# Releasing the second block's attention of a pair after the first part of that block's value projection

## The chip, the cores and the metric

The kernel runs on one core of a Trainium2 chip. Its time is the device time in microseconds (us) of one execution; the figure for a kernel is the median of its runs. The core has five engines that run their own instruction queues in order and wait for one another by semaphores: TensorE (PE in the profile, with PEld for its weight loads), VectorE (DVE), ScalarE (ACT), GpSimd (POOL) and SyncE (SP), which here issues the DMA transfers.

## The reference

One decoder block on 2048 tokens with 1024 features. Sliding-window attention and an mLSTM branch run side by side on one combined projection, then comes a SwiGLU feed-forward part. Cut to what matters here:

```python
h = modulate(rms_norm(x, g_pre_mix[l]), shift_m, scale_m)
proj = h @ w_in[l]
q_a, k_a, v_a, q_m, k_m, v_m, o_m, i_m, f_m, g_a, g_m = jnp.split(proj, split_points, axis=-1)
q_a = rope(q_a.reshape(B, S, N_Q_HEADS, HEAD_DIM), positions)      # 8 heads of 64
k_a = rope(k_a.reshape(B, S, N_KV_HEADS, HEAD_DIM), positions)     # 2 heads
y_a = sliding_window_attention(q_a, k_a, v_a, attn_sinks[l])       # window 128, blocks of 128
...
h_m = mlstm_chunkwise(q_m, k_m, v_m, i_pre, f_pre)
...
merged = sigmoid(g_a) * (y_a @ w_branch_attn[l]) + sigmoid(g_m) * (y_m @ w_branch_mlstm[l])
x = x + gate_m[:, None, :] * rms_norm(merged @ w_out[l], g_post_mix[l])
... # feed-forward part
```

In one attention block 128 queries meet the 128 keys of their own block and the 128 before:

```python
s = jnp.einsum('bnqhgd,bnkhd->bnhgqk', qb, kb)
m = jnp.maximum(jnp.max(s, axis=-1, keepdims=True), sink)
p = jnp.exp(s - m)
p = p / (jnp.sum(p, axis=-1, keepdims=True) + jnp.exp(sink - m))
o = jnp.einsum('bnhgqk,bnkhd->bnqhgd', p, vb)
```

## The kernel before

The tokens are cut into four blocks of 512, and these into two pairs. `superblock(sb)` writes the mixer part of one pair, with blocks b0 and b1; the feed-forward part follows after both pairs. Each operand of a large product is held as two terms, a rounded value and the rest, so that one product is three matmuls.

For each block three projections are made by `token_group`: q, kv (keys, values and gate inputs) and vm (the value rows of the mLSTM, function `vm`). A group yields four parts for vm; a part is 24 matmuls with 512 columns (128x512 in the profile, tile acc), and each of the four PSUM banks of the pool acc is evacuated when its 128 tokens are done (L819 for vm, L773 for q, L798 for kv), into tiles of the pool tx (nine buffers). Of the first pair's first block some steps are written in another function. After the projections of both blocks come the pair's other projections, `om`, `qk`, `ga`, `gm`, in a form with seven products for eight (tiles acc<-big,hl, with casts at L1588 on ACT and subtractions at L1589 on DVE), and then the outputs of b0 and of b1. The sums that this form needs of the hidden rows are made by `hsums` (casts L535 on ACT), of which one pair of sums is spawned before the projections of b1 and one behind them, by `start_f`.

Everything else is side work, written as generators ("streams") that yield how long they want to be left alone: `q_stream` and `k_stream` (transposes after the rotation, results stored to at_d in HBM), `gates(b)`, two attention streams, the convolution and the mLSTM chunks. While `run2` writes the matmuls of the parts, each advances an estimated clock `now[0]`, and `tick` lets each stream that is due write its next step:

```python
for _ in it.mms(made.pop(done)):
    if it.weave:
        tick()
```

A function among the items (`yield lambda: attend(b1)`) is called when `run2` comes to it. A scheduler then sets the final order of each engine's queue from this program, so the order on each engine is not simply the order of writing.

Attention of 128 tokens (`attention(n)`, n from 0 to 15, four to each block of 512) is: load the operands (L900, SP, at<-at_d; two buffers at), two groups of twelve score matmuls (L211, mix<-at, 64x256; two head groups on the two halves of PE's rows), copies to tm (L923, L925), exponentials on ACT (L938), a multiplication on POOL (L942), eight transposes (L216, mix<-ident,tm), four products with the values (L211, mix<-tm,at) and the store of the result. A bank of the pool mix (four) holds each of these results in PSUM. Two streams take the even and the odd attention blocks in turn; both may go on as far as `ready[0]` says:

```python
def attention_stream(u):
    for i in range(u, 2 * NT, 2):
        while i >= ready[0]:
            yield 1000.0
        yield from attention(b0 * NT + i)
...
def attend(b):
    finish(R["qk"])
    ready[0] = (b - b0 + 1) * NT
    if b == b0:
        R["att"] = [spawn(attention_stream(0), L_QK), spawn(attention_stream(1), L_QK + L_ATT2)]
    R["gs", b] = [spawn(gates(b), L_QK)]
```

So `attend(b1)` first has all steps written that the rotated q and k of b1 still owe, then lets the streams go on to the last four attention blocks of the pair (4 to 7, or 12 to 15), and spawns the gates of b1. The attention results of b1 are read after `end_attention(2 * NT)`, ahead of b0's output projection; the gates after the projection `qk` 3.

Of the kernel before, what the change touches and what calls it, by code (L numbers as in the profile page):

```python
# [72 lines left out]
def decoder_block(ctx: ExitStack, tc: tile.TileContext, a: dict, out: bass.AP, dbg=None):  # L73
# [49 lines left out]
    def tx(shape, dtype=F32):  # L123
        return tpool.tile(shape, dtype, tag="tx", name=nm("tx"), bufs=9)
# [93 lines left out]
    def spawn(gen, delay=0.0):  # L218
        st = [now[0] + delay, gen, False]
        streams.append(st)  # L220
        return st
# [15 lines left out]
    def finish(sts):  # L237
        for st in sts:
            while not st[2]:
                now[0] = max(now[0], min(q[0] for q in streams))  # L240
                tick()
# [75 lines left out]
    def token_group(srcs, nk, n, lhs, evac, pair_heads=False, stagger=1):  # L317

        acc = []
        srcs = list(srcs)  # L320
        held = []

        def make(si, k0, kc):
            def mms(wt):
                if not acc:
                    acc.extend(acc_tile() for _ in range(NT))
                held.append((wt, k0, kc))
                if len(srcs) - stagger <= si < len(srcs) - 1:
                    return
                for t in range(NT):  # L330
                    for w_, k0_, kc_ in held:
                        for j in range(kc_):
                            kk = k0_ + j
                            mm3(acc[t][:, :n], lhs(kk, t), (w_[0][:, j, :], w_[1][:, j, :]), kk == 0, kk == nk - 1)
                            yield
                    if si == len(srcs) - 1:
                        evac(t, acc[t])
                held.clear()
            return mms

        for si, (raw, view, k0, kc) in enumerate(srcs):
            yield piece(raw, view, [kc, n], make(si, k0, kc), pair_heads)

    def srcs_rows(w, nk, c0):
        for k0 in range(0, nk, 4):
            kn = min(4, nk - k0)
            raw = raw_rows(w, k0, kn, c0)
            for j in range(0, kn, 2):
                yield raw, (lambda t, j=j: t[:, j:j + 2, :]), k0 + j, 2
# [48 lines left out]
    b1 = const.tile([P, 48], F32, name="b1")  # L398
# [125 lines left out]
    def hsums(names):  # L524

        for name in names:
            raw = HR.pop(name)
            lo = hc_part(name, 1)
            nc.sync.dma_start(lo.bitcast(F32), raw)
        yield L_HD  # L530
        for name in names:
            hi, lo = (hc_part(name, i) for i in range(2))
            for k in range(4):
                v = lo[:, k, :].bitcast(F32)
                A.copy(hi[:, k, :], v)  # L535
                V.tensor_tensor(lo[:, k, :], v, hi[:, k, :].bitcast(F32), op=ALU.subtract)
                yield L_HS
# [190 lines left out]
    def superblock(sb):  # L728
        b0, b1 = 2 * sb, 2 * sb + 1
        R = {}  # L730

        def lhs_h(b):
            def lhs(kk, t):
                return tuple(p_[:, kk % 4, t * P:(t + 1) * P] for p_ in HC[f"{kk // 4 + 1}{b % 2 + 1}"])
            return lhs
# [80 lines left out]
        def vm(b):  # L816
            def evac(t, ps):
                v = tx([P, 512])
                A.copy(v, ps)  # L819
                nc.sync.dma_start(vm_d[b][:, t, :], v)  # L820
            yield from token_group(srcs_rows(w_in, KD, C_VM), KD, 512, lhs_h(b), evac)
# [149 lines left out]
# [5 lines that stand above are left out]
                done_att[0] += 1  # L976
                yield 500.0
# [3 lines left out]
# [6 lines that stand above are left out]
# [305 lines left out]
        q1, kv1 = (list(z) for z in q_kv(b1))  # L1292
        yield from kv1
        yield from q1
        yield from vm(b1)

        def start_f():
            finish([hps["t"]])
            HC.pop("12")
            hps["t"] = spawn(hsums(("T1", "T3")))  # L1300
            attend(b1)

        yield start_f
        pairs = [("om", 0), ("qk", 0), ("om", 1), ("qk", 1), ("ga", 0), ("qk", 2), ("ga", 1), ("qk", 3),
# [740 lines left out]
    def program():  # L2045
        items = [it for sb in range(NSB) for it in superblock(sb)]
        last = max(i for i, it in enumerate(items) if isinstance(it, Part))
        first_block()
        yield from items[:last]
        yield lambda: next(phase2)  # L2050
        yield from items[last:]
# [47 lines left out]
```

## Time and profile before

| | |
|---|---|
| median of 3 runs | 2695.2 us (2694.12 to 2695.24) |
| profiled execution | 2696.74 us, span 2695.0 us |
| mean granted clock of TensorE | 0.992 |
| busy: PE, DVE, ACT, POOL | 98%, 74%, 48%, 5% of the span |
| first pair, 190 to 560 us | PE busy throughout |
| second pair, 740 to 880 us | PE busy 126.94 of 140 us |

Rows of the timeline give the start and the time from the first start to the last end of a run of like instructions (us), engine, line, operation, output<-input, shapes and count; in brackets the idle time of the engine ahead of it and what ended it. Since matmuls overlap, a run's cost is the distance to the next start. Windows give busy times of each engine between two times, the granted clock (1.00 is full) and the share of time in which the 16 DMA engines were busy. Line numbers are those of the kernel before; behind line 1300 the changed kernel's are higher by 2.

### The profile page before, as it was taken

To read this page: it belongs to the slowest core of one execution; us is meant where nothing else is said; L and a number is where in the kernel's file an instruction comes from. 1 tells how busy PE (TensorE), PEld (TensorE's weight loads), DVE (VectorE), ACT (ScalarE), POOL (GpSimd) and SP (SyncE) were. 2 spreads that over 40 slices of the span, in tenths; PEclk is the share of its full clock that TensorE was granted. 3 is DMA by queue.
4 is the path that set the end of the run, shared out by engine and by line. 5 is a ranking of instruction groups with operands and counts; after the bars stand their busy time and mean duration, and the time that the engine had idled before them with its cause. 6 is when DMAs were issued, how large, how long until landed. Compare 5 with 4: busy or idle time off the path is not lost.

```text
span 2695.0 us, 35854 instructions
## 1 busy us (share of the span) xinstructions
PE 2635.9 (98%) x12382; PEld 2149.4 (80%) x12382; DVE 1986.3 (74%) x3882; ACT 1297.2 (48%) x2525; POOL 136.8 (5%) x181
## 2 busy tenths in 40 slices
PE   7899999999998999999999999999999999999998
PEld 6777788888885778888887888887877888888886
DVE  7888887768686888876687777776677676766466
ACT  4657544545754554444563443334554333333444
POOL 0100001100101000110000000000000000000000
PEclk9999999999998999999999999999999999999999
DMA  7574456897574644677775564436675232324566
GB/s 251 172 236 138 147 176 185 267 341 243 188 246 145 204 139 139 204 250 284 243 233 192 178 201 160 153 118 215 213 272 187 98 118 88 111 98 145 191 207 219
DMA packets 353637, 511.89 MB, mean 190 GB/s; under 512 B 25120, under 2 KB 213660, under 8 KB 348208
## 3 DMA queue, kind: packets, MB, share of 16 engines
q1 hardware_dynamic: 353288, 509.55, 57.2%
q8 instruction: 97, 1.59, 0.2%
q14 instruction: 84, 0.69, 0.1%
q10 hardware_dynamic: 168, 0.06, 0.0%
HBM read 357.12 MB, written 144.02 MB: 186 GB/s over the span
## 4 chain that ended last, share of the span: by engine, by line
PE 84%; DVE 6%; DMA 4%; ACT 2%; issue 1%; POOL 0%; SPq 0%; DVEq 0%; POOLq 0%; ACTq 0%
PE acc L211 59%; PE mix L211 22%; PE mix L216 2%; DVE hl L1589 1%; DMA at_d<-tx 1%; DMA raw<-as_d 1%; DMA tx<-in_w_ada_dram 1%; ACT hl L1588 1%; DMA at<-at_d 1%; DMA raw<-in_w_ffn_down_dram 1%; DVE wlo L267 0%; DMA raw<-ws_d 0%; DMA big<-big 0%; DVE tm L925 0%; DVE big L1589 0%
## 5 line engine op out<-in xcount | busy, mean ns | idle before, releaser
L211 PE MATMUL acc<-big,hl 128*128 128x512 f32 x3936 | 939.5, 393 | 2.3 <-ACT hl L1588 0.9
L211 PEld LDWEIGHTS acc<-big,hl 128*128 128x128 f32 x3936 | 732.8, 188 | 168.5 <-issue 9.0
L1588 ACT CAST hl<-raw 128x512 fp32r<-128x512 f32 x732 | 440.2, 621 | 494.9 <-PE acc L211 227.9
L1589 DVE TENSOR_TENSOR hl<-raw,hl 128x512 fp32r<-128x512 f32 x732 | 497.9, 696 | 196.5 <-ACT hl L1588 194.1
L211 PE MATMUL acc<-whi,big 128*128 128x512 f32 (+1 forms) x1216 | 356.2, 374 | 7.7 <-ACT tx L89 3.8
L211 PE MATMUL mix<-big,hl 128*128 128x512 f32 x1056 | 262.9, 390 | 1.7 <-ACT hl L1588 1.0
L211 PEld LDWEIGHTS acc<-whi,big 128*128 128x128 f32 x1216 | 222.0, 190 | 49.7 <-ACT tx L89 4.3
L211 PE MATMUL acc<-hl,hl 128*128 128x512 f32 x1008 | 237.3, 393 | 5.9 <-DVE hl L1589 3.3
L211 PEld LDWEIGHTS mix<-big,hl 128*128 128x128 f32 x1056 | 197.8, 188 | 44.4 <-ACT hl L1588 1.9
L211 PE MATMUL acc<-wlo,big 128*128 128x512 f32 (+1 forms) x608 | 225.9, 374 | 3.5 <-DVE wlo L267 3.5
L211 PEld LDWEIGHTS acc<-hl,hl 128*128 128x128 f32 x1008 | 187.0, 188 | 51.6 <-DVE hl L1589 8.7
L211 PE MATMUL mix<-hl,hl 128*128 128x512 f32 x792 | 182.3, 390 | 1.2 <-DVE ms L455 0.5
L211 PEld LDWEIGHTS mix<-hl,hl 128*128 128x128 f32 x792 | 148.0, 188 | 34.5 <-DVE hl L1589 2.9
L211 PE MATMUL acc<-big,whi 128*128 128x512 f32 x512 | 157.3, 393 | 0.0
L267 DVE TENSOR_TENSOR wlo<-raw,whi 128x1024 fp32r<-128x1024 f32 (+1 forms) x95 | 108.8, 1146 | 60.4 <-ACT whi L266 54.7
L266 ACT CAST whi<-raw 128x1024 fp32r<-128x1024 f32 (+1 forms) x95 | 93.7, 987 | 116.0 <-PE acc L211 104.7
L211 PEld LDWEIGHTS acc<-wlo,big 128*128 128x128 f32 x608 | 115.6, 190 | 24.1 <-DVE wlo L267 5.0
L457 POOL TENSOR_TENSOR rs<-ms,halves 128x1 f32<-128x1 f32 (+1 forms) x56 | 42.9, 779 | 1657.0 <-DVE ms L455 1647.2
L211 PE MATMUL mix<-hcT4h,hl 128*128 128x512 f32 x352 | 115.6, 389 | 0.7 <-ACT hl L1588 0.7
L211 PE MATMUL acc<-hcT2h,hl 128*128 128x512 f32 x352 | 115.5, 389 | 0.0
L211 PEld LDWEIGHTS acc<-big,whi 128*128 128x128 f32 x512 | 95.3, 188 | 19.2
L211 PE MATMUL acc<-big,wlo 128*128 128x512 f32 x256 | 97.5, 392 | 0.0
(350 smaller groups left out, 3544.2 us busy)
## 6 DMA issues: line engine op xcount, KB each, us to landing
raw<-in_w_in_dram SPq DMA_DIRECT2D x48, 1024.0 KB, 5.6
as_d<-w SPq DMA_DIRECT2D x154, 256.0 KB, 2.0
raw<-as_d SPq DMA_DIRECT2D x70, 512.0 KB, 3.9
raw<-in_w_ffn_gate_dram SPq DMA_DIRECT2D x22, 1024.0 KB, 5.7
raw<-in_w_ffn_up_dram SPq DMA_DIRECT2D x22, 1024.0 KB, 5.5
raw<-ws_d SPq DMA_DIRECT2D x40, 512.0 KB, 4.6
y_d<-tm SPq DMA_DIRECT2D x64, 256.0 KB, 3.7
tx<-in_w_ada_dram SPq DMA_DIRECT2D x64, 256.0 KB, 4.2
```

Of the source, the lines that this page charges most:

```text
L211: T.matmul(o, lhsT=lhsT, rhs=rhs, start=start, stop=stop, skip_group_check=resumed)
L216: T.transpose(o, i, ident[:k, :k])
L266: A.copy(hv, src)
L267: V.tensor_tensor(lv, src, hv.bitcast(F32), op=ALU.subtract)
L457: G.tensor_tensor(r[:, :n], ms[:, :n], nhalf[:, :n], op=ALU.pow)
L1588: A.copy(v(hi), src)
L1589: V.tensor_tensor(v(lo), src, v(hi).bitcast(F32), op=ALU.subtract)
```

## The change

`attend(b1)` is called after the first of the four parts of b1's vm, and no longer in `start_f`, which follows the fourth.

```diff
         yield from kv1
         yield from q1
-        yield from vm(b1)
+        vm1 = list(vm(b1))
+        yield from vm1[:len(vm1) // 4]
+        yield lambda: attend(b1)
+        yield from vm1[len(vm1) // 4:]
 
         def start_f():
             finish([hps["t"]])
             HC.pop("12")
             hps["t"] = spawn(hsums(("T1", "T3")))
-            attend(b1)
 
         yield start_f
```

The number of instructions on each engine stays; their order changes within both pairs, not in the feed-forward part. Three places follow, of before first and then of the changed kernel.

On PE in the first pair, at the first scores of attention block 4 (mix<-at). acc<-whi,big and acc<-wlo,big are matmuls of vm, acc<-big,hl those of the projections behind it:

```order
L211 MATMUL acc_1974<-whi_2063,big_993 128x512
L211 MATMUL mix_2253<-at_2156 128x256
L211 MATMUL mix_2254<-at_2156 128x256
...
L211 MATMUL mix_2253<-at_2156 128x256
L211 MATMUL acc_2145<-big_365,hl_2069 128x512
L211 MATMUL acc_2145<-big_378,hl_2069 128x512
L211 MATMUL mix_2254<-at_2156 128x256
L211 MATMUL acc_2145<-big_365,hl_2069 128x512 x2
```

```order
L211 MATMUL acc_1974<-whi_2035,big_993 128x512
L211 MATMUL acc_1971<-whi_2114,big_992 128x512
L211 MATMUL mix_2142<-at_2045 128x256 x4
L211 MATMUL mix_2143<-at_2045 128x256 x4
L211 MATMUL mix_2142<-at_2045 128x256
L211 MATMUL mix_2143<-at_2045 128x256
L211 MATMUL mix_2142<-at_2045 128x256
L211 MATMUL mix_2143<-at_2045 128x256
L211 MATMUL acc_1971<-wlo_2115,big_992 128x512
```

The twelve scores stood behind vm's last matmul, as eleven and one; they now stand together, 23 of vm's matmuls earlier.

On PE in the second pair, at the value products of attention block 8 (mix<-tm,at) and the transposes of block 9 (mix<-ident,tm):

```order
L211 MATMUL acc_8268<-whi_8356,big_7135 128x512
L211 MATMUL mix_7777<-tm_7755,at_7501 64x512
L216 MATMUL mix_7788<-ident,tm_7665 128x128
L211 MATMUL mix_7777<-tm_7770,at_7501 64x512
L216 MATMUL mix_7788<-ident,tm_7665 128x128 x2
L211 MATMUL mix_7777<-tm_7757,at_7501 64x512
L216 MATMUL mix_7788<-ident,tm_7665 128x128
L211 MATMUL mix_7777<-tm_7772,at_7501 64x512
L216 MATMUL mix_7805<-ident,tm_7666 128x128 x4
L211 MATMUL acc_8268<-wlo_8357,big_7135 128x512
```

```order
L211 MATMUL acc_8266<-wlo_8357,big_7135 128x512
L211 MATMUL mix_7777<-tm_7755,at_7501 64x512
L216 MATMUL mix_7788<-ident,tm_7665 128x128 x4
L216 MATMUL mix_7805<-ident,tm_7666 128x128 x2
L211 MATMUL mix_7777<-tm_7770,at_7501 64x512
L211 MATMUL mix_7777<-tm_7757,at_7501 64x512
L216 MATMUL mix_7805<-ident,tm_7666 128x128
L211 MATMUL mix_7777<-tm_7772,at_7501 64x512
L216 MATMUL mix_7805<-ident,tm_7666 128x128
L211 MATMUL acc_8266<-whi_8356,big_7136 128x512
```

Four single value products have become one, two and one, with all eight transposes among them, 14 of the projection's matmuls earlier.

On ACT at the start of the second pair: L819 evacuates vm of block 2, L535 are casts of `hsums`, L923 copies scores, L266 casts weights:

```order
L819 COPY tx_7908<-acc_7488 128x512
L789 CAST tx_7445<-mix_7482 128x128
L819 COPY tx_7979<-acc_7489 128x512
L923 COPY tm_7587<-mix_7589 128x256
L923 COPY tm_7588<-mix_7590 128x256
L535 CAST big_8083<-big_8023 128x512 x4
L923 COPY tm_7587<-mix_7607 128x256
L819 COPY tx_7991<-acc_7490 128x512
L266 CAST whi_8012<-raw_7461 128x528
L819 COPY tx_8009<-acc_7491 128x512
L535 CAST big_8164<-big_8025 128x512 x4
```

```order
L789 CAST tx_7445<-mix_7482 128x128
L819 COPY tx_7908<-acc_7488 128x512
L923 COPY tm_7587<-mix_7589 128x256
L923 COPY tm_7588<-mix_7590 128x256
L535 CAST big_8083<-big_8023 128x512 x4
L819 COPY tx_7979<-acc_7489 128x512
L923 COPY tm_7587<-mix_7607 128x256
L819 COPY tx_7991<-acc_7490 128x512
L535 CAST big_8164<-big_8025 128x512 x2
L266 CAST whi_8012<-raw_7461 128x528
L535 CAST big_8164<-big_8025 128x512 x2
L819 COPY tx_8009<-acc_7491 128x512
```

The second evacuation has moved behind the first four casts, and the fourth behind the other four.

## The prediction

> **What bounds the kernel now.** I read the page first, then windows around the places where the order of instructions differs, then the timeline of PE and ACT inside them. All durations come from the profiled execution: 2696.74 us, of which 2695.0 us is its span. The median of the runs before is 2695.2 us, 1.5 us less, so a sum made against 2696.74 us is carried over to 2695.2 us. What a measurement here can tell from no change is 0.2%, which is 5.4 us.
>
> The page gives the busy time of each engine and the shares of the chain that ended last:
>
> ```profile
> PE 2635.9 (98%) x12382; PEld 2149.4 (80%) x12382; DVE 1986.3 (74%) x3882; ACT 1297.2 (48%) x2525; POOL 136.8 (5%) x181
> PE 84%; DVE 6%; DMA 4%; ACT 2%; issue 1%; POOL 0%; SPq 0%; DVEq 0%; POOLq 0%; ACTq 0%
> ```
>
> PE is the bound. Of 2695 us only some 59 are free of PE work, so a change that only reorders can gain in three ways: fewer microseconds for the same PE work, shorter waits of PE, or less time at a reduced clock. The windows (columns: window, its length, busy time of PE, PEld, DVE, ACT and POOL with counts, granted clock, DMA share, GB/s) show how this stands at the places concerned:
>
> ```profile
> 190.00:210.00 20.00, 20.00 (x103) 15.74 (x102) 19.78 (x37) 12.45 (x25) 0.00 (x0) 1.00 0.96 364
> 330.00:560.00 230.00, 230.00 (x1168) 194.60 (x1167) 183.32 (x423) 105.61 (x198) 25.37 (x22) 1.00 0.69 221
> 836.00:859.00 23.00, 15.37 (x65) 8.19 (x66) 12.90 (x38) 13.51 (x50) 4.68 (x5) 0.70 0.31 87
> ```
>
> In the first pair PE has no gap from 190 to 210 us, nor from 330 to 560: there the release is worth only what it does to PE's own work. In the second pair a stretch of 23 us holds nothing but attention, PE works for 15.37 us of it, and the clock is 0.70: there waits count.
>
> **What the change moves.** No instruction is added or removed; the attention of a pair's second block enters three parts of 24 products earlier, and the scheduler then places differently all that interleaves. The differences lie in PE's program in the first pair from about 196 to 320 us and in the second from about 773 to 1240 us. I cost them by place.
>
> *Prices.* Two rows on PE set the price of a run of products. The counts in the rows are instructions; a run's cost is the distance to the next start:
>
> ```profile
> 201.68 0.97 PE L211 MATMUL mix<-at 64*128 64x256 f32 x11
> 202.58 0.73 PE L211 MATMUL acc<-big,hl 128*128 128x512 f32 x2
> 203.25 0.38 PE L211 MATMUL mix<-at 64*128 64x256 f32 x1
> 203.56 5.73 PE L211 MATMUL acc<-big,hl 128*128 128x512 f32 x24
> 209.22 0.74 PE L211 MATMUL mix<-at 64*128 64x256 f32 x8
> 209.89 1.65 PE L211 MATMUL acc<-big,hl 128*128 128x512 f32 x6
> 211.47 1.21 PE L211 MATMUL mix<-at 64*128 64x256 f32 x16
> 212.61 1.65 PE L211 MATMUL acc<-big,hl 128*128 128x512 f32 x6
> ```
>
> 24 products take 5.66 us (203.56 to 209.22) and 6 take 1.58 (209.89 to 211.47): 18 more cost 4.08, so one costs 0.227 us and each run 0.22 us beside its products. The score runs (mix<-at; each instruction uses one half of PE's rows) cost 0.90 for 11, 0.31 for 1, 0.67 for 8, 1.14 for 16. Other sizes:
>
> ```profile
> 945.35 0.97 PE L211 MATMUL mix<-at 64*128 64x256 f32 x6
> 946.24 0.50 PE L211 MATMUL acc<-big,hl 128*128 128x512 f32 x1
> 946.68 1.69 PE L211 MATMUL mix<-at 64*128 64x256 f32 x18
> 948.30 1.88 PE L211 MATMUL acc<-big,hl 128*128 128x512 f32 x7
> ```
>
> ```profile
> 894.71 1.69 PE L211 MATMUL mix<-at 64*128 64x256 f32 x24
> 896.33 1.89 PE L211 MATMUL acc<-big,hl 128*128 128x512 f32 x7
> ```
>
> Six of one row half alone cost 0.89, eighteen 1.62, and twenty-four also only 1.62: two halves run side by side when their instructions alternate, and one half alone wastes the other. Twelve cost 0.90 (below). The same holds for the product of probabilities and values (mix<-tm,at; the trace holds two records for each such instruction):
>
> ```profile
> 830.69 1.08 PE L211 MATMUL mix<-tm,at 128*64 128x512 f32 x4
> 831.70 0.50 PE L211 MATMUL acc<-wlo,big 128*128 128x512 f32 x1
> ...
> 833.07 0.97 PE L211 MATMUL mix<-at 64*128 64x256 f32 x12
> 833.97 1.07 PE L211 MATMUL mix<-tm,at 128*64 128x512 f32 x2
> 834.97 0.38 PE L211 MATMUL mix<-at 64*128 64x256 f32 x1
> ...
> 840.86 2.93 PE L211 MATMUL mix<-at 64*128 64x256 f32 x24 [3.37 <-DMA at<-at_d]
> ```
>
> ```profile
> 235.55 1.94 PE L211 MATMUL mix<-tm,at 128*64 128x512 f32 x8
> 237.41 1.66 PE L211 MATMUL acc<-big,hl 128*128 128x512 f32 x6
> ```
>
> One instruction alone costs 1.00 (833.97 to 834.97), two adjacent ones 1.01, four 1.86.
>
> *First pair, second block (attention blocks 4 to 7).* Score runs before: 11, 1, 8, 16, 12, 18, 6, 18, 6, together 8.9 us; after: 12, 24, 12, 24, 24, together 6.7. That is -2.3 us. The value products go from runs of 4, 1, 3, 4, 1, 2, 1 to 1, 7, 4, 1, 3, 9.7 us by the same prices both times. Term: **-2.3**. The first score comes 23 products (5.2 us) earlier, at about 196.4 instead of 201.68. Its operands are loaded by SP here, with the landing times of the loads of this pair below it:
>
> ```profile
> 187.91 0.32 SPq L900 DMA_DIRECT2D at<-at_d  x1
> ```
>
> ```profile
> DMA to landing us min/median/max: 5.8/6.0/6.2
> ```
>
> 187.91 + 6.2 is 194.1, so the load hides behind the products that still stand ahead, with 2.3 us to spare. If it came later, vm's products (24 and more) would be queued behind the score on PE; that belongs to the slower rival.
>
> *Second pair, second block (blocks 12 to 15).* Scores 12, 24, 12, 6, 12, 6, 18, 6 become 12, 24, 12, 24, 24: 8.6 to 6.7, -1.9. Value products 1, 2, 2, 2, 1, 1, 2, 1, 1, 2, 1 become 3, 5, 4, 1, 2, 1: 11.0 to 9.7, -1.3. Term: **-3.2**.
>
> *Second pair, first block.* Its scores (blocks 8 and 9) go from 18, 6, 12, 12 to 12, 6, 6, 6, 6, 12: **+1.0**.
>
> *Start of the second pair.* On ACT the second evacuation of vm's result (L819) stood ahead of four casts (L535) that wait for a transfer; now it stands behind them, and the fourth behind four more. The trace of before:
>
> ```profile
> 777.74 0.58 ACT L819 COPY tx<-acc 128x512 f32<-128x512 f32 x1 [4.10 <-DMA at_d<-tx]
> ...
> 781.11 2.18 ACT L535 CAST big<-big 128x512 fp32r<-128x512 f32 x4 [2.23 <-DMA big<-big]
> ...
> 783.46 0.58 ACT L819 COPY tx<-acc 128x512 f32<-128x512 f32 x1
> ...
> 784.47 0.59 ACT L819 COPY tx<-acc 128x512 f32<-128x512 f32 x1
> ```
>
> ```profile
> 784.10 0.39 PE L211 MATMUL acc<-whi,big 128*128 128x264 f32 x1 [2.93 <-ACT tx L819]
> ```
>
> Before, PE waited 2.93 us for the third evacuation and found the fourth done at 785.06. Now the casts end at 783.3, the second and third evacuation at about 783.8 and 784.6, and two casts, a weight cast and two more casts (some 2.7 us) put the end of the fourth at about 787.9, 2.8 us later. Queued behind it on PE are the products of the next projection. Ends: +1.0 (other work fills most of it) and +4.5 (all of it, and the clock price below). I take **+2.5**, near the full delay.
>
> *The attention-only stretch at 836.* It is entered when block 9's value products end (834.97), since block 11's operands go into the buffer that they free; PE then waits 3.37 us. In the new order 4 single value products of block 8 become 1, 2, 1 (-1.0), those of block 9 (1, 2, 1) stand together (-1.1), six products and twelve scores follow them instead of standing ahead (-1.4, -0.9), and two runs of products fewer stand ahead (-0.4): block 9 ends 4.8 us earlier, and what now follows fits into the 5.8 us that the next load takes. If the end of the stretch follows its start, that is -4.8; if it is set by evacuations that wait for tx buffers, 0. I take **-4.0**, since PE's work inside it is attention throughout.
>
> *Fewer interruptions.* Beside the stretches counted, runs of products become 4 fewer in the first pair and 16 fewer in the second (67 to 51): at most 20 x 0.22 = 4.4, at least 0, since a part may overlap. I take half: **-2.2**.
>
> *Where PE waits for the softmax.* The stall at 913 and its clock:
>
> ```profile
> 913.07 0.66 PE L216 MATMUL mix<-ident,tm 128*128 128x128 f32 x4 [1.43 <-POOL tm L942]
> ```
>
> ```profile
> 784.00:786.00 2.00, 1.90 (x12) 1.91 (x13) 2.00 (x4) 2.00 (x6) 0.00 (x0) 0.76 1.03 368
> 786.00:788.00 2.00, 2.00 (x12) 1.87 (x12) 1.94 (x6) 1.94 (x5) 0.00 (x0) 0.50 0.71 264
> 788.00:790.00 2.00, 2.00 (x18) 1.87 (x18) 2.00 (x7) 0.70 (x2) 0.00 (x0) 0.89 0.77 244
> ...
> 916.00:918.00 2.00, 2.00 (x6) 1.52 (x6) 0.34 (x2) 2.00 (x8) 1.40 (x2) 0.50 0.00 0
> ```
>
> A gap of PE costs twice: the wait, and then about 3.4 us at half clock, 2 x (0.24 + 0.50 + 0.11) = 1.7 us after the gap of 2.93. The gap of 1.43 is followed by 0.50 as well. In the new order these transposes stand 23 products later, so the 1.43 + 1.7 = 3.1 us could go; but ACT puts other casts between the exponentials of blocks 12 and 13, and the transposes of 13 follow at once. Ends -3.1 and +1.7; I take 0.
>
> The Trainium skill, "TensorE: Matmul & The Clock Gate", section "Part 1: The HAM clock gate", says that the clock falls to half after an idle window of about 3.4 us. By that rule neither the gap of 2.93 nor the one of 1.43 need have cost clock, and the new waits of the slower rival below would cost 11.7 instead of 18.4 us; the rows at 786 and 916 show 0.50 after both, so the trace decides otherwise.
>
> **Sum.** -2.3 - 3.2 + 1.0 + 2.5 - 4.0 - 2.2 = -8.2 us: 2696.7 becomes 2688.5, and from the median 2695.2 the forecast is **2687.0**. With every bound on the good side: -2.3 - 3.2 + 1.0 + 1.0 - 4.8 - 4.4 - 3.1 = -15.8, 2679.4. With every bound on the bad side and no new wait: -2.3 - 3.2 + 1.0 + 4.5 = 0.0, 2695.2.
>
> **Rivals.** *No change to speak of.* The stretch at 836 ends when the tx buffers come free, interruptions overlap, and the start of the second pair takes its 4.5 us: 2695.2. For it: PE's gaps are few and the output of the second block's attention is not read before the first block's output projection, which stands behind all the pair's other projections. To it belongs that the change hardly does what it says: only the first scores of blocks 4 and 12 come earlier, by 5 us, and the rest stays where evacuations and buffers put it. Against it: the score runs of one half alone are gone from the order. Chance 0.26.
>
> *Slower: attention in bunches meets its own softmax.* Scores now stand 24 together, transposes 8 or 12, value products 7. Where the products between a block's last scores and its transposes are shorter than its softmax, PE waits and then runs at half clock. The price is that of the gap at 784.10, 2.93 + 1.7 = 4.6 us; with one such wait at each of four places (blocks 4/5, 6/7, 12/13, 14/15) it is 18.4, and the sum becomes +10.2: 2705.4. It decides from three such waits on (13.8 - 8.2 = 5.6, just over what can be told). For it: the 836 stretch, where attention has no products beside it, shows PE at 15.37 of 23 us. A first score that meets its load still under way would be such a wait too. Against it: 25 to 60 products (6 to 14 us) still stand between, and the first pair has no gap now. Chance 0.28.
>
> *Larger gain.* The stall at 913 goes with its clock and the interruptions count in full: 2679.4. Against it: the order of ACT there. Chance 0.12.
>
> The forecast keeps 0.34. So faster by over 0.2% (under 2689.8) is 0.34 + 0.12 = 0.46, within 0.2% is 0.26, slower is 0.28. The range that holds 8 in 10 runs from 2680 to 2704: below lies a half of the larger gain, above about half of the slower rival. The likeliest case alone has 2682 to 2690.
>
> **What would show it.** Right: score runs of 6 alone gone from blocks 4 to 7 and 12 to 15; PE still full in the first pair, with its outputs some 3 us earlier; a wait for L819 at the start of the second pair that is longer than 2.93 us; the wait for at<-at_d near 841 starting some 2 to 5 us earlier relative to it. Wrong: the first pair no shorter (score runs priced wrongly), new waits of PE for L942 or at<-at_d in the first pair or after 877, or the stretch at 836 as long and as late as before.

## The result and the profile after

The changed kernel has a median of 2689.8 us over 11 runs (2680.65 to 2694.39), the kernel before 2694.7 us over 11 runs beside it; the ratio is 0.9972 with a 95% interval of 0.9960 to 0.9983, that is -7.5 us (-10.8 to -4.6). The forecast was -8.2 us. The profiled execution of the change took 2691.05 us, its span 2689.2 us against 2695.0. Two executions far longer than the others of their kernels, one of e6 (3039 us, mean granted clock 0.815) and one of e7 (15042 us), are left out of the ratios below.

The page and the windows of the changed kernel, beside those of before in the prediction:

```profile
PE 2630.6 (98%) x12382; PEld 2149.5 (80%) x12382; DVE 1986.7 (74%) x3882; ACT 1297.4 (48%) x2525; POOL 138.1 (5%) x181
```

```profile
190.00:210.00 20.00, 20.00 (x114) 16.17 (x115) 19.79 (x37) 12.82 (x25) 0.00 (x0) 1.00 0.97 358
330.00:560.00 230.00, 230.00 (x1168) 194.57 (x1167) 184.16 (x421) 105.01 (x199) 25.36 (x22) 1.00 0.69 221
836.00:859.00 23.00, 16.09 (x86) 8.66 (x85) 12.42 (x37) 14.58 (x52) 4.16 (x4) 0.85 0.42 131
```

PE's busy time fell by 5.3 us with the same 12382 matmuls: what is gone is work of PE, not waiting. To see where, I took the same product (the n-th matmul that writes acc) in both traces; the difference of its start times is how far the change is ahead there. Between such points it gained or lost:

| time in before, us | place | forecast | measured |
|---|---|---|---|
| 185 to 346 | first pair, blocks 4 to 7 | -2.3, and a part of -2.2 for fewer interruptions | -1.7 |
| 346 to 730 | | 0 | 0.0 |
| 730 to 773 | weights of the second pair's first projections | 0 | +3.9 |
| 773 to 795 | start of the second pair, scores of 8 and 9 | +2.5 + 1.0 | +3.6 |
| 795 to 859 | stretch with nothing but attention | -4.0 | -5.0 |
| 859 to 1011 | blocks 12 to 15, gap at 913 | -3.2, gap 0 | -8.2 |
| 1011 to 1272 | mLSTM beside the projections | the rest of -2.2 | +2.3 |
| 1272 to the end | same order | 0 | -1.0 |

A piece of one profile also carries chance. Up to 185 us the order on PE is the same in all thirteen traces, and yet at that point they lie between 4.9 us ahead of before (e2) and 2.7 us behind it (e9). Where several kernels have the same order in a piece, they are compared below.

Within these pieces I summed the distances from each matmul to the next by kind, with PE's gaps taken out, for this profile and those of the experiments; the sums are used below as "work of PE".

In the first pair the two groups of attention on PE read, before and after (columns: shapes, count, then the time in which at least one of them ran, their mean in ns, idle time ahead):

```profile
L211 PE MATMUL mix<-tm,at 128*64 128x512 f32 x32 | 10.1, 610 | 0.0
L211 PE MATMUL mix<-at 64*128 64x256 f32 x96 | 9.6, 293 | 0.0
```

```profile
L211 PE MATMUL mix<-tm,at 128*64 128x512 f32 x32 | 9.7, 605 | 0.0
L211 PE MATMUL mix<-at 64*128 64x256 f32 x96 | 7.0, 289 | 0.0
```

The same 96 scores are done in 7.0 instead of 9.6 us, at the same mean duration of one: the two row halves overlap more often. The timeline of PE after:

```profile
196.52 0.98 PE L211 MATMUL mix<-at 64*128 64x256 f32 x12
...
270.93 3.05 PE L211 MATMUL acc<-big,hl 128*128 128x512 f32 x12 [1.52 <-ACT tx L1737]
```

The first score came at 196.52 (forecast 196.4) without a wait for its load, 23 products earlier. The rest of the attention did not follow it. Counted in products of acc done before a block's first score, block 5 comes 6 products earlier, but blocks 6 and 7 come 12 and 13 later; in the second pair block 12 comes 17 earlier, block 13 one later, blocks 14 and 15 come 28 and 30 later. What the early release changed is above all which pieces stand together.

Then a wait appeared that before had not. The evacuation L1737 (L1735 in before) stands on ACT right behind the eight exponentials of block 7 and started at 270.31, about as late as before (270.06). PE came to its bank some 2.6 us earlier than before and waited 1.52 us for it.

### The profile page after: what moved, and what is told of

Read it like the earlier page. It is cut to its first block, busy times and chain, and to the rows that moved or that the text cites. A ratio compares the mean times of both kernels' runs of the same rounds, so it can differ in the third digit from the quotient of the medians.

```text
span 2689.2 us, 35838 instructions
## 1 busy us (share of the span) xinstructions
PE 2630.6 (98%) x12382; PEld 2149.5 (80%) x12382; DVE 1986.7 (74%) x3882; ACT 1297.4 (48%) x2525; POOL 138.1 (5%) x181
## 4 chain that ended last, share of the span: by engine, by line
PE 84%; DVE 6%; DMA 3%; ACT 2%; issue 2%; POOL 0%; SPq 0%; DVEq 0%; POOLq 0%; ACTq 0%
PE acc L211 59%; PE mix L211 23%; PE mix L216 2%; DVE hl L1591 1%; DMA raw<-as_d 1%; ACT hl L1590 1%; DMA at<-at_d 1%; ACT tm L938 0%; DVE wlo L267 0%; DMA big<-big 0%; DVE tm L925 0%; DMA tx<-in_w_ada_dram 0%; DMA big<-in_x_dram 0%; DMA raw<-in_w_ffn_down_dram 0%; DVE mx L930 0%
## 5 line engine op out<-in xcount | busy, mean ns | idle before, releaser
L266 ACT CAST whi<-raw 128x1024 fp32r<-128x1024 f32 (+1 forms) x95 | 93.8, 987 | 131.0 <-PE acc L211 122.9
```

The costliest lines, as they stand in the source:

```text
L266: A.copy(hv, src)
```

## The experiments

Comparisons are with the kernel before, run on the same chip (one chip for e1 to e4, one for e5 to e8, one for e9 to e11); changes in us are the ratio times before's median there.

**Which pair.** e1 to e3, e7, e8, e10 and e11 differ only in how many of vm's four parts stand ahead of the release, by pair; 4 means in `start_f`, as before:

```diff
-        yield from vm1[:len(vm1) // 4]
-        yield lambda: attend(b1)
-        yield from vm1[len(vm1) // 4:]
+        early = (1, 4)[sb]              # e1; e2 (4, 1), e3 (2, 1), e7 (0, 0),
+        yield from vm1[:early]          # e8 (3, 3), e10 (2, 0), e11 (2, 3)
+        if early < 4:
+            yield lambda: attend(b1)
+        yield from vm1[early:]
...
             hps["t"] = spawn(hsums(("T1", "T3")))
+            if early == 4:
+                attend(b1)
```

> The early release in the first pair alone; the second pair keeps the release behind vm. This order also carries the changed start of the second pair (the second and fourth evacuation L819 behind the casts L535). Theory (the gain comes from the second pair's blocks 12 to 15): the first pair's outputs 1.6 us earlier, the start of the second pair 5 us dearer, the stretch at 836 4.9 us shorter, and the gap at 913 of 1.43 us is there: together -1 to -2 us, not to be told from no change. Rival (the gain comes from the first pair's scores and the stretch): -5 to -8 us.

Measured: ratio 0.9991 (0.9979 to 1.0003), -2.4 us, 2690.3 against 2694.4 us by the medians. First pair -1.8 us in its trace, with the same wait of 1.51 us for the evacuation. Not to be told from no change, as the theory had it.

> The early release in the second pair alone. The start of the second pair is as before. Theory: no change up to 870 us; the blocks 12 to 15 give some 8 us until 1000, of which 2 are lost until 1250: about -6 us, 2689. The wait for L942 at 913 is gone. Rival: within 2 us of before.

Measured: 0.9976 (0.9965 to 0.9987), -6.5 us. The gap for L942 at 913 is gone. So most of the gain belongs to the second pair; the rival that set it in the first pair and the stretch falls.

> First pair: release after two of the four parts of vm; second pair: after one, as in the change. The order of the start of the second pair is that of before (the second L819 ahead of the casts). Theory: first pair about -2 us, no loss at the start of the second pair and no shorter stretch, blocks 12 to 15 as in e2: -7 to -8 us. Rival (start of the second pair and stretch belong together and their sum is what the change gains): -3 us or less.

Measured: 0.9973 (0.9959 to 0.9986), -7.3 us. First pair -3.0 us by the trace: work of PE as in the change, and no wait for the evacuation.

**Which part of the release.** e4 leaves the gates in `start_f`, e5 leaves the attention there:

```diff
-        yield lambda: attend(b1)
+        yield lambda: (finish(R["qk"]), ready.__setitem__(0, 2 * NT))                # e4
+        yield lambda: (finish(R["qk"]), R.update({("gs", b1): [spawn(gates(b1), L_QK)]}))  # e5
...
             hps["t"] = spawn(hsums(("T1", "T3")))
+            R.update({("gs", b1): [spawn(gates(b1), L_QK)]})                          # e4
+            ready.__setitem__(0, 2 * NT)                                              # e5
```

> In both pairs only the attention streams are released early; the gates of the second block are spawned behind vm, as before. Scores stand in runs of 12 and 24 in blocks 4 to 7 and 12 to 15 as in the change, the start of the second pair is as before. Theory (the gain is attention's own): -7 us, 2688. Rival (the early gates bring the gain, since the mLSTM's steps wait for them): within 2 us of before.

Measured: 0.9992 (0.9981 to 1.0004), -2.2 us. A miss. Its scores are as cheap as in the change (6.7 us of PE in the first pair), but with the gates late the value products fall apart there (10.8 us instead of 9.3), and between 1011 and 1272 us PE waits 2.8 us where the change waits 1.1 and before nothing.

> In both pairs only the gates of the second block (and the outstanding steps of its q and k) come after the first part of vm; its attention is released behind vm, as before. Score runs and value runs of the second pair stand as before, also its start. Theory (attention's own placement brings the gain): within 2 us of before. Rival (the gates bring the larger part, since releasing attention alone gave only 2 us): -4 to -6 us.

Measured: 1.0002 (0.9991 to 1.0013), +0.5 us. The gates alone bring nothing; released with the attention they change where its pieces stand. Neither part has the gain to itself.

**Whether the time of release matters.**

> Release ahead of vm instead of after its first part, in both pairs. Score runs as in the change; value products of the second pair 3, 5, 1, 2, 2, 2, 1 instead of 3, 5, 4, 1, 2, 1, and 6 runs of products more: by the prices +0.2 and +1.3 us. Theory (what counts is how the pieces stand on PE, not how early the release is): -5 to -7 us, no better than the change. Rival (the earlier the better): -9 us or more.

Measured: 0.9962 (0.9947 to 0.9976), -10.2 us, a little more than forecast and, by its interval, not to be told from the change.

> Release after three of the four parts of vm, in both pairs. Score runs as in the change but for an 11 and 1 at the start of the first pair; value products of the second pair 1, 2, 3, 1, 1, 1, 2, 1, 1, 2, 1, by the prices +2.2 us, and 10 runs of products more, +2.2 us. Theory: -3 us. Rival (a third of the advance gives a third of the gain): -2.5 us; these two are told apart by the trace alone: by the first, blocks 4 to 7 are as fast as in the change and blocks 12 to 15 lose 4 us against it.

Measured: 0.9964 (0.9951 to 0.9976), -9.7 us. Three times as much as the theory's prices gave, and as much as e7 with a release 72 products earlier. By the trace blocks 12 to 15 do cost more than in the change, 94.4 instead of 93.1 us from 911 to 1011; but nothing is lost between 1011 and 1272 (260.4 us; before 260.2, change 262.5). The size of the advance therefore does not set the gain: 24 products earlier give as much as 96. Part of e8's gain may be the clock: its runs had a mean granted clock of 0.9933, those of before beside them 0.9920, which by the line in the last section is some 3 us. A release after the fourth part but ahead of `start_f`'s other steps was not run.

> First pair: release after two parts of vm; second pair: ahead of vm. First pair as in e3 (-3 us, no wait for the evacuation near 271), start and stretch of the second pair as in e3, blocks 12 to 15 with runs as in the change and six runs of products more than e3. Theory: between the change and e7, -7 to -10 us. Rival (earlier is better in the second pair): better than -11 us.

Measured: 0.9985 (0.9974 to 0.9996), -4.0 us.

> First pair: release after two parts of vm; second pair: after three. First pair as in e3 (-3 us); start and stretch as in e3; blocks 12 to 15 with more single value products, but nothing lost between 1011 and 1272 us, as in e8. Theory: -7 to -10 us, like e8. Rival (e8's gain hangs on the start of the second pair that only it and the change have): -4 us or less.

Measured: 0.9981 (0.9971 to 0.9991), -5.1 us. Both are less than the theory gave; by the intervals their distance from e7 and e8 is at the edge of what can be told. What they lack in the traces against e7 and e8 is the other order of blocks 8 and 9, which comes with 0, 1 or 3 parts in the first pair but not with 2: from 795 to 859 they take 64.3 us, before 64.2, the change 59.2, e7 and e8 60.4. So the rival of e11 has its point: the order at the start of the second pair, which I had put down as a loss, brings the shorter stretch. In the times this doesn't stand out: e2 and e3 have the order of before there as well and gained 6.5 and 7.3 us; in their traces PE waits 1.7 and 1.8 us at the start of the second pair, where before waits 2.93, with no half clock after it (-2.2 us from 773 to 795). Part of e10's shortfall may be the clock (0.9913 in its runs, 0.9921 in before's beside them, nearly 2 us by the same line).

**Whether the runs on PE set the price.** e9 keeps the release behind vm and takes one yield out of `attention`, which happens to tear the value products apart:

```diff
-                if jj == 0:
-                    yield 0
```

> The kernel before (release behind vm) with one yield between the two halves of an attention block's scores taken out. Its order breaks up the value products: in blocks 4 to 7 runs of 1, 1, 1, 1, 2, 1, 1, 2, 1, 1, 3, 1 instead of 4, 1, 3, 4, 1, 2, 1, in blocks 12 to 15 ones, two twos and a three instead of ones and six twos; the scores there cost 0.8 us less in each. Theory (prices of runs on PE decide where PE has no gap): 3.3 - 0.8 in the first pair and 3 - 0.8 in the second, +4 to +5 us. Rival (the time of release decides): no change.

Measured: 1.0028 (1.0015 to 1.0041), +7.5 us. The groups of the first pair in its trace:

```profile
L211 PE MATMUL mix<-tm,at 128*64 128x512 f32 x32 | 13.7, 616 | 0.0
L211 PE MATMUL mix<-at 64*128 64x256 f32 x96 | 9.5, 299 | 0.0
```

The 16 value products (two records each) take 13.7 us where they took 10.1; as work of PE 12.9 instead of 9.6, the +3.3 that the prices gave. In blocks 12 to 15 they take 13.9 instead of 11.1. The time of the release is that of before, so the cost comes from the order alone. The scores of the first pair, forecast 0.8 us cheaper, cost 8.8 us instead of 9.0. The whole is some 3 us over the +4 to +5, but its interval (4.0 to 11.1 us) holds the forecast.

**Whether a gap costs a second time by the clock.** e6 is the changed kernel with 14 matmuls into the bank that the scores of block 11 overwrite:

```diff
                     banks[g, jj] = mix_tile()
+                if jj == 0 and n in (11,):
+                    for _ in range(14):
+                        T.matmul(banks[0, 0][:, :P], lhsT=ident, rhs=ident, start=True, stop=True)
```

> The changed kernel with 14 extra matmuls (identity by identity, 128x128, some 0.16 us each, 2.2 us in all) written ahead of the scores of attention block 11 into the bank that these then overwrite; the order of everything else on PE is that of the change. They fill most of the wait of 3.0 us for at<-at_d near 843. Theory (a gap of PE costs twice, the second time by the clock): the extra matmuls cost nothing and the half clock of two spans of 3.4 us in 843 to 860 shrinks, -1 to -3 us against the changed kernel, mean clock higher by about 0.001. Rival (the low clock there does not come from this gap): within 1 us of the changed kernel.

Measured: 0.9967 (0.9954 to 0.9980), -8.9 us against before, where the change has 0.9972: 1.4 us more, as the theory had it, but far within the intervals, so the times do not decide. PE's timeline in the changed kernel and in e6 (whose lines behind 914 are 3 higher):

```profile
833.90 1.94 PE L211 MATMUL mix<-tm,at 128*64 128x512 f32 x8
835.77 1.69 PE L211 MATMUL mix<-at 64*128 64x256 f32 x18
...
838.97 0.97 PE L211 MATMUL mix<-at 64*128 64x256 f32 x6
842.96 1.69 PE L211 MATMUL mix<-at 64*128 64x256 f32 x24 [3.03 <-DMA at<-at_d]
...
853.02 0.66 PE L216 MATMUL mix<-ident,tm 128*128 128x128 f32 x4 [1.20 <-POOL tm L942]
854.61 0.93 PE L216 MATMUL mix<-ident,tm 128*128 128x128 f32 x4 [0.94 <-POOL tm L942]
```

```profile
835.52 3.39 PE L916 MATMUL mix<-ident 128*128 128x128 f32 x28
838.85 1.70 PE L211 MATMUL mix<-at 64*128 64x256 f32 x24
...
848.82 0.66 PE L216 MATMUL mix<-ident,tm 128*128 128x128 f32 x4 [2.67 <-POOL tm L945]
850.41 0.65 PE L216 MATMUL mix<-ident,tm 128*128 128x128 f32 x4 [0.93 <-POOL tm L945]
```

The filler covered the wait for the load, and the half clock did shrink: the granted clock from 836 to 859 us is 0.93 in e6, 0.85 in the change. But from those scores to block 11's last transposes it is 11.6 us in e6 and 11.7 in the change: what PE did faster it waited longer for POOL (2.67 instead of 1.20). Up to there the chain over DVE, ACT and POOL sets the length, and half clock on PE is hidden.

Behind those transposes it is not hidden. Before and e2 have the same order on PE here; before runs it at half clock at first (0.50 from 854 to 856 us), e2 at full clock (1.00 from 848 to 852):

```profile
853.77 1.12 PE L216 MATMUL mix<-ident,tm 128*128 128x128 f32 x4 [0.90 <-POOL tm L942]
854.81 1.97 PE L211 MATMUL mix<-tm,at 128*64 128x512 f32 x2
...
859.03 0.48 PE L211 MATMUL acc<-whi,big 128*128 128x512 f32 x1
```

```profile
848.04 0.66 PE L216 MATMUL mix<-ident,tm 128*128 128x128 f32 x4 [0.90 <-POOL tm L942]
848.62 1.07 PE L211 MATMUL mix<-tm,at 128*64 128x512 f32 x2
...
851.94 0.48 PE L211 MATMUL acc<-whi,big 128*128 128x512 f32 x1
```

From the transposes to the next product it is 5.26 us in before and 3.90 in e2. The change and e6 both have half clock here and take 5.44 and 5.48. So the filler removed a span of half clock that was hidden, and e6 does not show that a gap costs nothing by the clock elsewhere.

## Why the prediction was right, point by point

**The price of the runs was right.** Scores of blocks 4 to 7 cost 9.0 us of PE before and 6.7 after, the forecast -2.3. Those of blocks 12 to 15 went from 5.2 to 3.2 in the piece from 911 to 1011 (-2.0, forecast -1.9), their value products from 11.1 to 9.5 (-1.6, forecast -1.3). e9 is the test from the other side. In the first pair before has no gap on PE, so there the price goes straight into the time.

**The interruptions were mis-sized.** I took 0.22 us for each run of products and then half of the bound. In the first pair 7 runs fewer saved 0.8 us of products (137.0 to 136.2), 0.11 each; from 1011 to 1272 us 9 fewer saved 0.7. The 0.22 was read from runs next to scores and may have counted in part a cost that the score prices held already; that was not tested. And the piece that should have gained lost 2.3 us: 1.1 in waits that were not there, 1.1 in the small matmuls of the mLSTM (27.1 to 28.2) and 0.8 in transposes, which now stood elsewhere. I had looked only at how often products were interrupted, not at what the interrupting pieces cost in their new places.

**The start of the second pair came out at +3.6 for +3.5 by luck, not by the step as told.** ACT did what the order said:

```profile
781.98 2.18 ACT L535 CAST big<-big 128x512 fp32r<-128x512 f32 x4 [5.64 <-DMA big<-big]
784.06 0.57 ACT L819 COPY tx<-acc 128x512 f32<-128x512 f32 x1
...
784.81 0.59 ACT L819 COPY tx<-acc 128x512 f32<-128x512 f32 x1
...
787.90 0.60 ACT L819 COPY tx<-acc 128x512 f32<-128x512 f32 x1
```

```profile
784.69 0.59 PE L211 MATMUL acc<-whi,big 128*128 128x264 f32 x1 [2.88 <-ACT tx L819]
```

Yet PE waited 2.88 us, no longer than the 2.93 before: it now needed the second evacuation there, and other products and six scores covered the wait for the fourth. The loss came from the clock, in the changed kernel and in e1, which has the same order there:

```profile
784.00:786.00 2.00, 1.31 (x6) 1.31 (x7) 1.94 (x7) 2.00 (x6) 0.00 (x0) 0.50 1.06 381
786.00:788.00 2.00, 2.00 (x13) 2.00 (x12) 1.94 (x5) 2.00 (x5) 0.00 (x0) 0.50 0.87 310
788.00:790.00 2.00, 2.00 (x10) 1.76 (x9) 2.00 (x5) 0.77 (x3) 0.00 (x0) 0.50 0.72 206
790.00:797.00 7.00, 7.00 (x31) 6.31 (x30) 5.48 (x14) 1.38 (x3) 0.00 (x0) 0.51 0.34 100
```

```profile
780.00:784.00 4.00, 3.21 (x17) 3.21 (x18) 3.88 (x11) 4.00 (x10) 0.00 (x0) 0.57 1.03 384
784.00:797.00 13.00, 13.00 (x103) 12.11 (x101) 11.85 (x31) 6.40 (x14) 0.00 (x0) 1.00 0.56 183
```

PE and ACT have the same order up to there in both, and the wait is the same (2.85 us in e1): one profile has half clock until 797, the other is back at 784 and lost nothing against before there (-0.5 us between the same products). Of the other kernels with this order at the place, e6 had the long half clock of 13.7 us again (+4.0 us), e7 and e8 the short one of 3.4 (-0.3 and -0.8), as long as before's own. So this term is no price of the order: it differs between profiles of the same order, and with the half clock of before it is about 0.

**The stretch went as forecast**, -5.0 for -4.0: block 9's value products stand together (833.90, x8) and what follows them fits into the wait for the load. Cut at block 11's last transposes, the traces show the price of the order without the clock. From 795 to those transposes the order of before takes 58.7 us in six profiles that have it on PE (before, e2, e3, e4, e10, e11) and 59.3 in the seventh (e5), the changed order 53.5 to 53.9 us in all five (the change, e1, e6, e7, e8): some 5 us. From there to the next product it is 3.9 to 6.5 us with either order, as half clock falls there or not, which is why e7 and e8 show only -3.8 over the whole stretch. The wait at 842.96 is 3.03 us where I had it at 5.8 less the work put behind.

**The gap at 913** I took as 0 between -3.1 and +1.7; it went altogether, and the transposes that it held up run without a wait:

```profile
917.64 0.60 PE L216 MATMUL mix<-ident,tm 128*128 128x128 f32 x4
...
918.31 1.04 PE L216 MATMUL mix<-ident,tm 128*128 128x128 f32 x8
...
919.98 0.66 PE L216 MATMUL mix<-ident,tm 128*128 128x128 f32 x4
```

But e1, whose blocks 12 to 15 are ordered as in before, shows what belongs to the profiled execution alone:

```profile
906.44 0.66 PE L216 MATMUL mix<-ident,tm 128*128 128x128 f32 x4 [0.39 <-POOL tm L942]
```

0.39 instead of 1.43 us, and no half clock after it; from 859 to 1011 it is 3.9 us ahead of before with its scores and value products as in before; e5, of which the same holds, 2.8. Of the -8.2 in the table some 3 to 4 are thus before's own bad luck, and 4 to 5 the change.

**The rivals.** The slower one did not come: in the first pair its waits stayed at one of 1.52 us, without half clock after it, a third of the price given, and the first scores found their loads landed. "No change" was right that little but the first scores of blocks 4 and 12 moves to an earlier place; it was wrong that the time hangs on this, since the runs that the pieces make changed all the same. The forecast came out within 1 us in part by luck. A loss that I had not foreseen (the clock and a wait of 2.46 us for weights near 735, against 0.44 in before; in the other profiles this piece is between 0.4 us shorter and 2.9 longer) stood against a gain at 913 that I had left at 0. With before's own chances taken out, the pieces are -1.7 in the first pair, about 0 at the start of the second, -5 in the stretch, -4 to -5 in blocks 12 to 15 and +2.3 behind them: without the piece at 735 some -8.5 to -9.5 us, where -7.5 (-10.8 to -4.6) was measured. Between the parts of the sum there is luck, between the prices of PE's runs there is not.

**What stays open.** e1 has the -1.7 of the first pair and the -5 of the stretch in its trace, but its runs gained only 2.4 us, by their interval at most 5.7; where its runs lose the rest was not found. Why e8 gains as much as e7 is shown only in part (the stretch, nothing lost after 1011, and perhaps the clock); why one profile has the short half clock and another the long one after the same gap was not found; why the place of the gates decides how the value products stand (e4) comes out of the scheduler and was not followed. None of the variants is shown to beat the change: the intervals of e7 and e8 overlap its own.

## What to carry to other kernels

Where PE has no gaps, price a reordering by the runs that it makes: small matmuls that use half the array cost as much alone as in pairs, so what keeps the pairs adjacent is gain; how much earlier something is released is none by itself. Before a gap of the profile enters a sum, compare it with the same place in a second execution or a kernel that is unchanged there. And count for pieces that are pushed elsewhere what they cost in their new place.

## What the runs showed of the hardware

The clock after a gap is no fixed price. After the same gap of 2.8 to 2.9 us in the same order it was at half for 13.7 us in the change and in e6, with PE busy almost throughout (the rows from 784 to 797), and for 3.4 us in e1 and e7. The Trainium skill, "TensorE: Matmul & The Clock Gate", section "Part 1: The HAM clock gate", says that what is issued in the first 3.4 us or so runs at half clock and everything after at full; the rows of the changed kernel (0.50 until 797, with PE back at 784.69) differ from that, those of e1 agree. Nor does the length of the gap alone decide: the wait of 1.43 us at 913 in before was followed by half clock, the one of 1.52 us at 270 in the change was not (1.00 from 268 to 276 us), and neither were those of 1.7 and 1.8 us at the start of the second pair in e2 and e3. Over 35 runs of the kernel before, the time falls by 2.2 us for each 0.001 of mean granted clock (a straight line through them gives 2689.3 us at 0.995 and 2700.3 us at 0.990); the correlation is -0.75, so a good half of the variance of one kernel's runs goes with the clock. The mean clock of the change's runs was no higher than before's (0.9920 over 11 runs, 0.9925 over those 35), so its gain is not one of clock.
